# Gate and up as a 2x2 block product with seven products, and weight tiles of three k-tiles, in a streamed fp32 decoder layer

## The chip, the cores and the metric

The kernel runs on one core of a Trainium2 chip. The metric is the time of one execution in microseconds of the device; the time before is the median of three runs.

## The reference

One decoder layer on x of 256 tokens by 2048, all in fp32, with alpha = 2^(1/4):

```
x <- LN1(alpha*x + 0.5*SwiGLU_1(x))                  # D_FF = 5632
x <- LN2(alpha*x + W_out [DiffAttn(x @ W_in) || RWKV7(x @ W_in)])   # W_in: 2048 x 6432
x <- LN3(alpha*x + 0.5*SwiGLU_2(x))
swiglu(x, wg, wu, wd) = (silu(x @ wg) * (x @ wu)) @ wd
```

Almost all of the arithmetic is in the matrix products with w_gate, w_up (2048 x 5632 each), w_down (5632 x 2048), twice, and W_in and W_out.

## The kernel before

Tokens stand in two tiles of 128, called token tile 0 and 1 (`tt` in the code). An activation tile is transposed on PE and split into a high half in the reduced format fp32r and the remainder (`xh`, `xl`), and so is each weight tile (`wh`, `wl`). A product of a k-tile (128 rows of K) with a column block of 512 is three matmuls into one PSUM bank: xh*wh, xh*wl, xl*wh (L113, L114, L115).

Weights pass through once. A step of `Stream.block` loads two k-tiles of one column block (`raw`, 128x1024, on SP's DMA queue, L134), ACT rounds them to `wh` (L137), DVE subtracts to get `wl` (L138), and PE uses them first for token tile 0 and then, LAG steps later (4 in the FFNs, 2 in the mixer), for token tile 1. There are three `raw` buffers, and seven slots of `wh` and `wl` in the FFNs, five in the mixer. `raw` and five of these slots live in a pool `wp` that all stages share.

The stages are FFN1, the mixer ("mix") and FFN2. An FFN has eleven column blocks of gate and up, in halves of six and five. For each, a gate block is followed by an up block; `gate_done` takes Silu of the gate's bank on ACT (`sg`, L222), `up_done` multiplies on DVE (`h`, L227), PE transposes h (L230) and ACT and DVE split it (`hh`, L240, L241). After each half the down product runs over its k-tiles for four column blocks, and `down_done` adds into `y` (L264, L266). When a token tile's last block is there, `ln_tail` normalises it in four quarters on DVE (L193, L194); in the first two stages each quarter is transposed and split for the next stage (L75, L81, L82) and written to a DRAM tile `xs` on ACT's queue (L199), and in the last it goes to the output. The mixer begins with a block of 288 columns of W_in, and its attention and recurrence run beside the weight stream as background generators; its final product is with W_out.

Nothing in the code fixes the order of work on an engine: a scheduler that simulates the program when it is built sets each engine's order, and the pools' buffers decide which instruction has to wait for which.

## Time and profile before

| | |
|---|---|
| median of three runs | 2006.51 us (2006.06 to 2007.28) |
| profiled execution: its own span | 2006.8 us |
| PE busy | 1972.1 us (98%), 9671 matmuls |
| DVE busy | 1145.7 us (57%) |
| ACT busy | 885.0 us (44%) |
| DMA | 373.35 MB, mean 186 GB/s |

Busy times count an engine's own instructions and not those that only issue DMAs. A matmul's record is longer than the distance to the next one, since matmuls overlap; what one costs is the distance between starts. The page names the instruction that released a waiting one, and the chain is followed back from the end in this way.

### The profile page before, as it was taken

How to read it: one execution, taken by the hardware profiler on the slowest of the kernel's cores; microseconds unless marked ns; L12 is line 12 of the kernel's file. 1: busy time of each engine (PE TensorE's matmuls, PEld its weight loads, DVE VectorE, ACT ScalarE, POOL GpSimd, SP SyncE). 2: the span in 40 equal slices, each digit the busy share in tenths (PEclk: the TensorE clock that was granted, in tenths of full speed). 3: DMA queues.
4: the chain of work that ended last, by engine and by line, in shares of the span. 5: the costliest groups of instructions: out<-in, count | busy, mean ns of one | idle time of the engine just before them, and what ended most of it. 6: DMA issues, size and time to landing. Idle time of an engine off the chain costs nothing.

```text
span 2006.8 us, 24924 instructions
## 1 busy us (share of the span) xinstructions
PE 1972.1 (98%) x9671; PEld 1618.6 (81%) x9671; DVE 1145.7 (57%) x1419; ACT 885.0 (44%) x1096; POOL 34.2 (2%) x68
## 2 busy tenths in 40 slices
...
GB/s 243 220 188 189 187 191 206 211 192 230 190 188 189 195 167 192 155 160 171 137 123 147 187 117 171 210 200 189 189 188 190 206 211 191 230 190 188 190 195 128
DMA packets 202008, 373.35 MB, mean 186 GB/s; under 512 B 22826, under 2 KB 24944, under 8 KB 201120
## 3 DMA queue, kind: packets, MB, share of 16 engines
...
## 4 chain that ended last, share of the span: by engine, by line
PE 91%; DVE 4%; DMA 2%; ACT 1%; issue 1%; ACTq 0%; POOL 0%; DVEq 0%
PE acc L113 28%; PE acc L115 28%; PE acc L114 28%; DVE wl L138 1%; DMA raw<-in_ffn_w_gate_dram 1%; PE tr L230 1%; ACT wh L137 1%; DVE y L193 1%; DVE y L194 1%; PE sm L556 0%; PE tr L353 0%; DMA raw<-in_ffn_w_up_dram 0%; PE pr L498 0%; PE at L775 0%; PE tr L75 0%
## 5 line engine op out<-in xcount | busy, mean ns | idle before, releaser
L138 DVE TENSOR_TENSOR wl<-raw,wh 128x1024 fp32r<-128x1024 f32 (+1 forms) x665 | 807.9, 1217 | 649.1 <-ACT wh L137 648.4
L137 ACT CAST wh<-raw 128x1024 fp32r<-128x1024 f32 (+1 forms) x665 | 694.9, 1047 | 832.7 <-PE acc L115 728.3
L115 PE MATMUL acc<-wh,xl 128*128 128x512 f32 (+1 forms) x1952 | 740.6, 391 | 0.5 <-DVE xl L82 0.5
L114 PE MATMUL acc<-wl,xh 128*128 128x512 f32 (+1 forms) x1952 | 735.4, 392 | 3.9 <-DVE wl L138 3.9
L113 PE MATMUL acc<-wh,xh 128*128 128x512 f32 (+1 forms) x1952 | 728.1, 392 | 0.3 <-ACT xh L81 0.2
L114 PEld LDWEIGHTS acc<-wl,xh 128*128 128x128 f32 x1952 | 368.0, 189 | 80.0 <-DVE wl L138 5.2
L113 PEld LDWEIGHTS acc<-wh,xh 128*128 128x128 f32 x1952 | 368.2, 189 | 79.1 <-issue 3.0
L115 PEld LDWEIGHTS acc<-wh,xl 128*128 128x128 f32 x1952 | 367.8, 188 | 77.0 <-issue 2.3
L115 PE MATMUL acc<-wh,hh 128*128 128x512 f32 x704 | 254.5, 390 | 0.0
L114 PE MATMUL acc<-wl,hh 128*128 128x512 f32 x704 | 253.6, 389 | 0.0
L113 PE MATMUL acc<-wh,hh 128*128 128x512 f32 x704 | 252.6, 389 | 0.0
L114 PEld LDWEIGHTS acc<-wl,hh 128*128 128x128 f32 x704 | 132.1, 188 | 27.6
L115 PEld LDWEIGHTS acc<-wh,hh 128*128 128x128 f32 x704 | 132.2, 188 | 27.4
L113 PEld LDWEIGHTS acc<-wh,hh 128*128 128x128 f32 x704 | 132.1, 188 | 27.4
L241 DVE TENSOR_TENSOR hh<-tr,hh 128x512 fp32r<-128x512 f32 x44 | 30.4, 691 | 64.2 <-ACT hh L240 64.2
L240 ACT CAST hh<-tr 128x512 fp32r<-128x512 f32 x44 | 25.8, 586 | 91.2 <-PE tr L230 91.2
L227 DVE SCALAR_TENSOR_TENSOR h<-sg,acc 128x512 f32<-128x512 f32 x44 | 30.2, 687 | 34.9 <-PE acc L115 34.9
L222 ACT ACTIVATE sg<-acc 128x512 f32<-128x512 f32 x44 | 26.3, 598 | 42.9 <-PE acc L115 42.9
L230 PEld LDWEIGHTS tr<-ident,h 128*128 128x128 f32 x176 | 21.7, 140 | 6.3 <-DVE h L227 0.7
L230 PE MATMUL tr<-ident,h 128*128 128x128 f32 x176 | 26.4, 272 | 0.3 <-DVE h L227 0.3
L584 DVE TENSOR_TENSOR itmp<-U,Y 64x31 f32<-64x31 f32 (+15 forms) x62 | 20.5, 331 | 7.3 <-DMA U<-dU 5.9
L586 DVE TENSOR_TENSOR Y<-Y,itmp 64x31 f32<-64x31 f32 (+15 forms) x62 | 20.6, 332 | 1.4
...
## 6 DMA issues: line engine op xcount, KB each, us to landing
raw<-in_ffn_w_up_dram SPq DMA_DIRECT2D x176, 512.0 KB, 3.8
raw<-in_ffn_w_down_dram SPq DMA_DIRECT2D x176, 512.0 KB, 4.2
raw<-in_ffn_w_gate_dram SPq DMA_DIRECT2D x175, 512.0 KB, 3.9
raw<-in_w_in_dram SPq DMA_DIRECT2D x96, 512.0 KB, 3.7
raw<-in_w_out_dram SPq DMA_DIRECT2D x32, 512.0 KB, 4.2
xs<-y ACTq DMA_DIRECT2D x16, 256.0 KB, 3.1
rc<-xs ACTq DMA_DIRECT2D x16, 256.0 KB, 4.3
...
```

Source lines behind the costliest of these rows:

```text
L113: T.matmul(a, hi, wh[:, j, :w], start=(ki + j == 0), stop=False)
L114: T.matmul(a, hi, wl[:, j, :w], start=False, stop=False)
L115: T.matmul(a, lo, wh[:, j, :w], start=False, stop=(ki + j == last))
L137: SC.copy(out=wh[:, c, :w], in_=raw[:, c, :w])
L138: V.tensor_tensor(out=wl[:, c, :w], in0=raw[:, c, :w], in1=wh[:, c, :w].bitcast(F32), op=ALU.subtract)
L222: SC.activation(out=s, in_=acc, func=AF.Silu)
L227: V.scalar_tensor_tensor(out=h, in0=sg[tt], scalar=0.5, in1=acc, op0=ALU.mult, op1=ALU.mult)
L230: T.transpose(tr[:, i, :], h[:, i * P:(i + 1) * P], ident)
L240: SC.copy(out=hi, in_=tr)
L241: V.tensor_tensor(out=lo, in0=tr, in1=hi.bitcast(F32), op=ALU.subtract)
L584: V.tensor_tensor(out=tv, in0=U[:, 0:j, j:j + 1].to_broadcast([64, j, 32 - j]), in1=Y[:, j:j + 1, j:32].to_broadcast([64, j, 32 - j]), op= ...
L586: V.tensor_tensor(out=Y[:, 0:j, j:32], in0=Y[:, 0:j, j:32], in1=tv, op=ALU.add)
```

## The change

For every column block of an FFN but the first, `two_blocks` computes gate and up together. On k-tiles 0 to 5 it takes the 2x2 block product of (token tile 0, 1) x (k-tiles 0 to 2, 3 to 5) with (k-tiles 0 to 2, 3 to 5) x (gate, up) in the form with seven products instead of eight. Its operands are differences of weight tiles, made in place on the loaded tiles by DVE (L172, L176, L177, L188), and four sums and differences of the x tiles (`xsh`, `xsl`), made once in an FFN by `combinations` (L284 to L292). Sums of products are made in PSUM: bank `u` begins as a copy of `a` (L174) and `w` as a copy of `u` (L181), both by ACT; `z` is copied to SBUF as `s5` (L180) and DVE adds it to `u` in place (L184) and to `w` to give `v` (L186). The other ten k-tiles run as before into the four banks, `a` and `w` for the gate, `u` and `v` for up.

Around it, weight tiles are three k-tiles wide (128x1536) in the FFNs, apart from each FFN's first gate block; token tile 1 follows one step behind; there are four slots of `wh` and `wl` and eight of `raw`; `raw`, `wh` and `wl` live in each stage's own pool, so in the mixer and FFN2 they lie over tiles of the stage before; there are six accumulator banks and two for transposes; gamma and beta of the FFNs' norms are loaded into the tiles of x of token tile 1.

```diff
-LAG = {"ffn": 4, "mix": 2}
-NW = {"ffn": 7, "mix": 5}
-NRAW = 3
+LAG = {"ffn": 1, "mix": 2}
+NW = {"ffn": 4, "mix": 5}
+NRAW = {"ffn": 8, "mix": 3}
+WIDE = {"ffn": 3, "mix": 2}
+NACC = {"ffn": 6, "mix": 3}
...
-    wp = ctx.enter_context(tc.tile_pool(name="wp", bufs=1))
...
+        def load(self, src, r0, n, c0, w=NB, g=None):
+            raw = self.pool.tile([P, self.wide, NB], F32, tag="raw", name=nm("raw"), bufs=NRAW[self.name])
...
+        def halves(self, raw, n, w=NB, g=None):
...
+                SC.copy(out=wh[:, c, :w], in_=raw[:, c, :w])
+                V.tensor_tensor(out=wl[:, c, :w], in0=raw[:, c, :w], in1=wh[:, c, :w].bitcast(F32), op=ALU.subtract)
...
+        def two_blocks(self, srcs, c0, x, comb, done):
+            self.flush()
+            s0, s1 = srcs
+            a, z, u, w, v = (self.bank() for i in range(5))
+            A11, A12, A21, A22 = ((lambda j, t=t, k=k: x(t, k + j)) for t in range(2) for k in (0, 3))
+            r11 = self.load(s0, 0, 3, c0)
+            self.product(a, A11, 3, *self.halves(r11, 3), True, False)
+            r12 = self.load(s1, 0, 3, c0)
+            V.tensor_tensor(out=r11, in0=r12, in1=r11, op=ALU.subtract)
+            self.product(z, comb(0), 3, *self.halves(r11, 3), True, True)
+            SC.copy(out=u, in_=a)
+            r22 = self.load(s1, 3, 3, c0)
+            V.tensor_tensor(out=r12, in0=r22, in1=r12, op=ALU.subtract)
+            V.tensor_tensor(out=r11, in0=r22, in1=r11, op=ALU.subtract)
+            self.product(u, comb(1), 3, *self.halves(r11, 3), False, False)
+            s5 = self.pool.tile([P, NB], F32, tag="s5", name=nm("s5"))
+            SC.copy(out=s5, in_=z)
+            SC.copy(out=w, in_=u)
+            r21 = self.load(s0, 3, 3, c0)
+            self.product(a, A12, 3, *self.halves(r21, 3), False, False)
+            V.tensor_tensor(out=u, in0=u, in1=s5, op=ALU.add)
+            self.product(w, comb(2), 3, *self.halves(r12, 3), False, False)
+            V.tensor_tensor(out=v, in0=w, in1=s5, op=ALU.add)
+            self.product(u, comb(3), 3, *self.halves(r22, 3), False, False)
+            V.tensor_tensor(out=r11, in0=r21, in1=r11, op=ALU.subtract)
+            rest = [(6, 3), (9, 3), (12, 2), (14, 2)]
+            for i, (src, banks) in enumerate(((s0, (a, w)), (s1, (u, v)))):
+                for k, n in rest:
+                    raw = self.load(src, k, n, c0)
+                    h = self.halves(raw, n)
+                    for t in range(2):
+                        if i == 0 and k == 6 and t == 1:
+                            self.product(w, A22, 3, *self.halves(r11, 3), False, False)
+                        self.product(banks[t], lambda j: x(t, k + j), n, *h, False, k == 14)
+                        if k == 14:
+                            done(i, t, banks[t])
...
-                stream.block(wg, c0, NB, KX, x_lhs, gate_done)
-                stream.block(wu, c0, NB, KX, x_lhs, lambda tt, acc, j=j: up_done(tt, acc, j))
+                if j0 + j == 0:
+                    stream.block(wg, c0, NB, KX, x_lhs, gate_done, 2)
+                    comb = combinations()
+                    stream.block(wu, c0, NB, KX, x_lhs, lambda tt, acc, j=j: up_done(tt, acc, j))
+                    stream.flush()
+                else:
+                    stream.two_blocks((wg, wu), c0, x_lhs, comb, lambda i, tt, acc, j=j: up_done(tt, acc, j) if i else gate_done(tt, acc))
...
-                gb = load_gb(fp, lg, lb, "lng", "lnb", hT[(0, 0)][0][:, 0, 0:1].bitcast(F32))
+                gb = load_gb_over_x(lg, lb)
```

How the order of the engines changes is shown at three places. In the rows, the number behind a tile's name tells its buffers apart, and a wait names the engine or DMA queue whose semaphore is waited for.

PE in a gate block of FFN1 before; acc_224 is token tile 0's bank of one block, acc_238 the bank of the next:

```order
L113 MATMUL acc_238_1255<-wh_243_1287,xh_22_164 128x512 [waits Activation_49]
L113 MATMUL acc_224_1186<-wh_229_1212,xh_49_286 128x512
L114 MATMUL acc_224_1186<-wl_230_1213,xh_49_286 128x512
L115 MATMUL acc_224_1186<-wh_229_1212,xl_50_287 128x512
L113 MATMUL acc_224_1186<-wh_229_1212,xh_49_286 128x512
L114 MATMUL acc_224_1186<-wl_230_1213,xh_49_286 128x512
L114 MATMUL acc_238_1255<-wl_244_1288,xh_22_164 128x512 [waits DVE_49]
L115 MATMUL acc_238_1255<-wh_243_1287,xl_23_165 128x512
```

PE in the seven products after; acc_254 is the bank u, acc_255 the bank w, and the wait for ACT at w's first matmul is for the copy of u into w (L181), which itself waits for the row above it:

```order
L130 MATMUL acc_254_1410<-wh_264_1449,xsh_58_327 128x512
L131 MATMUL acc_254_1410<-wl_265_1450,xsh_58_327 128x512
L132 MATMUL acc_254_1410<-wh_264_1449,xsl_59_328 128x512
L130 MATMUL acc_255_1411<-wh_270_1481,xsh_58_327 128x512 [waits Activation_49]
L131 MATMUL acc_255_1411<-wl_271_1482,xsh_58_327 128x512 [waits DVE_49]
L132 MATMUL acc_255_1411<-wh_270_1481,xsl_59_328 128x512
```

Before, matmuls of two banks alternate where an operand is late; after, the nine matmuls of w stand directly behind the last of u.

DVE in the gate and up stage before:

```order
L138 TENSOR_TENSOR wl_327_1725<-raw_325_1723,wh_326_1724 128x1024 [waits DMAHW3_49,Activation_49]
L138 TENSOR_TENSOR wl_331_1744<-raw_329_1742,wh_330_1743 128x1024 [waits DMAHW4_49,Activation_49]
L227 SCALAR_TENSOR_TENSOR h_322_1707<-sg_294_1557,acc_298_1571 128x512 [waits PE_49]
L138 TENSOR_TENSOR wl_334_1762<-raw_332_1760,wh_333_1761 128x1024 [waits DMAHW5_49,Activation_49]
L138 TENSOR_TENSOR wl_337_1780<-raw_335_1778,wh_336_1779 128x1024 [waits DMAHW6_49,Activation_49]
L241 TENSOR_TENSOR hh_324_1714<-tr_323_1709,hh_324_1714 128x512 [waits Activation_49]
L138 TENSOR_TENSOR wl_343_1808<-raw_341_1806,wh_342_1807 128x1024 [waits DMAHW7_49,Activation_49]
```

DVE in the seven products after, from the second low half of a pair to the addition of s5 to u; raw_257, raw_260, raw_263 and raw_267 are the tiles r11, r12, r22 and r21, and the two h belong to the pair before:

```order
L123 TENSOR_TENSOR wl_262_1432<-raw_257_1413,wh_261_1431 128x1536 [waits Activation_49]
L305 SCALAR_TENSOR_TENSOR h_246_1382<-sg_232_1294,acc_198_1104 128x512 [waits PE_49]
L177 TENSOR_TENSOR raw_257_1413<-raw_263_1445,raw_257_1413 128x1536 [waits DVE_49]
L305 SCALAR_TENSOR_TENSOR h_249_1398<-sg_233_1302,acc_200_1106 128x512 [waits PE_49]
L123 TENSOR_TENSOR wl_269_1468<-raw_267_1465,wh_268_1467 128x1536 [waits DMAHW6_49,Activation_49]
L123 TENSOR_TENSOR wl_265_1450<-raw_257_1413,wh_264_1449 128x1536 [waits Activation_49]
L123 TENSOR_TENSOR wl_271_1482<-raw_260_1428,wh_270_1481 128x1536 [waits PE_49,Activation_49]
L188 TENSOR_TENSOR raw_257_1413<-raw_267_1465,raw_257_1413 128x1536 [waits DVE_49]
L123 TENSOR_TENSOR wl_273_1496<-raw_263_1445,wh_272_1495 128x1536 [waits PE_49,Activation_49]
L319 TENSOR_TENSOR hh_248_1389<-tr_247_1384,hh_248_1389 128x512 [waits Activation_49]
L319 TENSOR_TENSOR hh_251_1405<-tr_250_1400,hh_251_1405 128x512 [waits Activation_49]
L184 TENSOR_TENSOR acc_254_1410<-acc_254_1410,s5_266_1462 128x512 [waits Activation_49]
```

Before, low halves alternate with the h and hh of the pair before; after, differences of weight tiles and an addition in PSUM stand among them, and the next nine matmuls of u (PE) wait for the last row.

SP's queue at the border from FFN1 to the mixer before:

```order
L134 DMA raw_973_5300<-in_ffn1_w_down_dram 128x2x512 [waits DMAHW5_49,DVE_49]
L134 DMA raw_1006_5467<-in_w_in_dram 128x2x288 [waits DMAHW6_49,DVE_49]
L134 DMA raw_1010_5480<-in_w_in_dram 128x2x288 [waits DMAHW7_49,DVE_49]
L134 DMA raw_1013_5492<-in_w_in_dram 128x2x288 [waits DMAHW0_49,DVE_49]
L134 DMA raw_1017_5511<-in_w_in_dram 128x2x288 [waits DMAHW1_49,DVE_49]
L134 DMA raw_1020_5529<-in_w_in_dram 128x2x288 [waits DMAHW3_49,DMAHW2_49,DVE_49]
```

SP's queue at the same place after; raw_886 lies over token tile 0's y and raw_890 over token tile 1's, and the DMA queues that these two rows wait for are those of the writes of xs0 and of xs1:

```order
L114 DMA raw_853_5053<-in_ffn1_w_down_dram 128x3x512 [waits DMAHW2_49,DVE_49]
L114 DMA raw_886_5208<-in_w_in_dram 128x2x288 [waits DMAHW1_49,DMAHW2_49,DMAHW0_49,DMAHW7_49,DVE_49,PE_49]
L114 DMA raw_890_5221<-in_w_in_dram 128x2x288 [waits DMAHW4_49,DMAHW5_49,DMAHW3_49,DMAHW6_49,DVE_49,PE_49]
L114 DMA raw_893_5233<-in_w_in_dram 128x2x288
L114 DMA raw_897_5252<-in_w_in_dram 128x2x288 [waits DMAHW7_49,DVE_49]
L114 DMA raw_900_5270<-in_w_in_dram 128x2x288 [waits DMAHW0_49,DVE_49]
```

Before, the first loads of W_in wait only for buffers of the weight stream; after, they stand behind the end of each token tile's norm and the writes of its result. On PE the matmuls of W_in's first block come after all 32 transposes of the two token tiles, where before they were mixed with them.

At the border to FFN2, PE before, from the first transposes of token tile 0's y:

```order
L75 MATMUL at_1909_10044<-ident_76,y_1707_9153 128x128 [waits DVE_49]
L75 MATMUL at_1909_10044<-ident_76,y_1707_9153 128x128 x3
L75 MATMUL sm_1912_10056<-ident_76,y_1707_9153 128x128 [waits DVE_49,PE_49]
L75 MATMUL sm_1912_10056<-ident_76,y_1707_9153 128x128 x3
L113 MATMUL acc_1944_10185<-wh_1942_10180,xh_1910_10049 128x512 [waits Activation_49]
L75 MATMUL at_1915_10068<-ident_76,y_1708_9154 128x128 [waits DVE_49]
L75 MATMUL at_1915_10068<-ident_76,y_1708_9154 128x128 x3
L75 MATMUL sm_1918_10080<-ident_76,y_1708_9154 128x128 [waits DVE_49,PE_49]
L75 MATMUL sm_1918_10080<-ident_76,y_1708_9154 128x128 x3
L114 MATMUL acc_1944_10185<-wl_1943_10181,xh_1910_10049 128x512 [waits DVE_49]
L115 MATMUL acc_1944_10185<-wh_1942_10180,xl_1911_10050 128x512 [waits DVE_49]
L113 MATMUL acc_1944_10185<-wh_1942_10180,xh_1910_10049 128x512
```

and after, from the last transposes of token tile 1's y:

```order
L76 MATMUL sm_1808_9874<-ident_73,y_1587_8894 128x128 [waits DVE_49,PE_49]
L76 MATMUL sm_1808_9874<-ident_73,y_1587_8894 128x128 x3
L76 MATMUL at_1811_9886<-ident_73,y_1588_8895 128x128 [waits DVE_49,PE_49]
L76 MATMUL at_1811_9886<-ident_73,y_1588_8895 128x128 x3
L76 MATMUL sm_1814_9898<-ident_73,y_1588_8895 128x128 [waits DVE_49,PE_49]
L76 MATMUL sm_1814_9898<-ident_73,y_1588_8895 128x128 x3
L130 MATMUL acc_1822_9924<-wh_1820_9920,xh_1790_9790 128x512 [waits Activation_49]
L130 MATMUL acc_1826_9943<-wh_1820_9920,xh_1806_9867 128x512
L131 MATMUL acc_1822_9924<-wl_1821_9921,xh_1790_9790 128x512 [waits DVE_49]
L132 MATMUL acc_1822_9924<-wh_1820_9920,xl_1791_9791 128x512
L130 MATMUL acc_1822_9924<-wh_1820_9920,xh_1790_9790 128x512
L131 MATMUL acc_1822_9924<-wl_1821_9921,xh_1790_9790 128x512
```

Before, matmuls of FFN2's first gate block follow the first transposes of token tile 0; after, the first of them follows the last transposes of token tile 1, and the second waits for a low half (wl_1821) that stands on DVE behind seven of the combinations of x.

127 lines of the change are left out of this document (79 added, 48 removed).

## The prediction

> **What bounds the kernel now.** I read the page's busy shares and its chain first, then a table of stretches, then the timeline of each engine at the stage borders. The page's busy line, with the share of the span in brackets, and the chain by engine and line:
>
> ```profile
> PE 1972.1 (98%) x9671; PEld 1618.6 (81%) x9671; DVE 1145.7 (57%) x1419; ACT 885.0 (44%) x1096; POOL 34.2 (2%) x68
> PE 91%; DVE 4%; DMA 2%; ACT 1%; issue 1%; ACTq 0%; POOL 0%; DVEq 0%
> ```
>
> PE is the path, so a matmul taken away shortens the span unless something new stands in its place. The stretches below are a gate/up stretch of FFN1, the border from FFN1 to the mixer, the mixer, the border to FFN2, and the tail (stretch and its length, then busy us of PE, PEld, DVE, ACT, POOL, granted clock, DMA share, GB/s):
>
> ```profile
> 100.00:270.00 170.00, 170.00 (x765) 140.66 (x764) 85.11 (x77) 73.55 (x78) 0.00 (x0) 1.00 0.66 189
> 730.00:760.00 30.00, 25.30 (x137) 22.18 (x136) 24.08 (x43) 9.79 (x16) 2.04 (x2) 0.89 0.46 146
> 760.00:1240.00 480.00, 470.65 (x2949) 377.12 (x2949) 340.40 (x634) 258.68 (x441) 11.23 (x12) 0.98 0.53 156
> 1240.00:1270.00 30.00, 26.17 (x104) 20.41 (x103) 28.34 (x42) 9.39 (x11) 2.00 (x2) 0.83 0.58 175
> 1990.00:2006.80 16.80, 4.85 (x22) 3.69 (x20) 12.32 (x20) 0.00 (x0) 2.01 (x2) 0.80 0.38 125
> ```
>
> In gate/up PE never waits, with DVE half idle and DMA at two thirds; time is lost only at borders and ends. So the change takes work off the bound, and what counts is what it puts in PE's way.
>
> **1. Matmuls removed.** A gate/up pair before is 16 k-tiles x 2 token tiles x 2 matrices x 3 = 192 matmuls. After, six k-tiles take 7 products of 9 (63 for 72), so 183. Twenty pairs (two FFNs, eleven each, the first of each left as it was): 180 fewer. Two neighbouring pairs' h on DVE, and eight transposes in a row on PE, give the price:
>
> ```profile
> 139.05 0.69 DVE L227 SCALAR_TENSOR_TENSOR h<-sg,acc 128x512 f32<-128x512 f32 x1 [1.31 <-PE acc L115]
> 183.54 0.69 DVE L227 SCALAR_TENSOR_TENSOR h<-sg,acc 128x512 f32<-128x512 f32 x1 [1.31 <-PE acc L115]
> 740.90 1.03 PE L75 MATMUL tr<-ident,y 128*128 128x128 f32 x8
> ```
>
> (183.54 - 139.05 - 1.03) / 192 = 0.2264 us a matmul; 180 x 0.2264 = **-40.8 us**, 2.04 a pair. All of it lies on the path.
>
> **2. What stands in its place in each pair.** Rows for the new work (line, engine, shapes, count, busy us, mean ns, idle before); the second row serves for back-to-back work, the third is an add out of PSUM, the fourth a 384-wide operation:
>
> ```profile
> L138 DVE TENSOR_TENSOR wl<-raw,wh 128x1024 fp32r<-128x1024 f32 x655 | 800.7, 1224 | 648.7 <-ACT wh L137 648.0
> L194 DVE SCALAR_TENSOR_TENSOR y<-y,rs,lnb 128x512 f32<-128x512 f32 x24 | 16.7, 747 | 0.0
> L266 DVE TENSOR_TENSOR y<-y,acc 128x512 f32<-128x512 f32 x16 | 10.9, 684 | 17.0 <-PE acc L115 17.0
> L777 DVE SCALAR_TENSOR_TENSOR s<-dist,at 128x384 f32<-128x384 f32 x16 | 8.4, 544 | 2.4 <-PE at L775 2.4
> L137 ACT CAST wh<-raw 128x1024 fp32r<-128x1024 f32 x655 | 688.2, 1052 | 816.4 <-PE acc L115 718.1 <-DMA raw<-in_ffn_w_gate_dram 31.8 <-DMA raw<-in_ffn_w_up_dram 26.1
> L349 ACT COPY tm<-acc 128x512 f32<-128x512 f32 x20 | 11.7, 587 | 10.3 <-PE acc L115 10.1
> ```
>
> 512 columns more cost DVE 1.224 - 0.684 = 0.54, so a 128x1536 instruction is put at 1.77 on DVE, and on ACT at 1.05 + (1.05 - 0.59) = 1.5.
>
> *The copy w<-u (L181).* PE's queue has the nine matmuls of w right behind the last of u. The copy can't begin before that last matmul is out, nor w before the copy. The end of the kernel shows the first latency (PE's last matmul of token tile 0, DVE's use of it), and that border of FFN2 the second (wl's end at 1262.11, PE's start):
>
> ```profile
> 1987.66 0.39 PE L115 MATMUL acc<-wh,hh 128*128 128x512 f32 x1
> 1988.09 0.69 DVE L266 TENSOR_TENSOR y<-y,acc 128x512 f32<-128x512 f32 x1 [5.62 <-PE acc L115]
> 1994.46 0.39 PE L115 MATMUL acc<-wh,hh 128*128 128x512 f32 x1
> 1995.24 0.68 DVE L266 TENSOR_TENSOR y<-y,acc 128x512 f32<-128x512 f32 x1
> 1999.69 2.73 DVE L194 SCALAR_TENSOR_TENSOR y<-y,rs,lnb 128x512 f32<-128x512 f32 x4
> 1260.90 1.21 DVE L138 TENSOR_TENSOR wl<-raw,wh 128x1024 fp32r<-128x1024 f32 x1
> 1262.17 0.80 PE L114 MATMUL acc<-wl,xh 128*128 128x512 f32 x1 [0.55 <-DVE wl L138]
> ```
>
> 0.43 from start to reader, 0.59 copy, 0.06 to PE, less the 0.23 that a matmul takes anyway: 0.85 us idle a pair. Unseen is a copy with both ends in PSUM: as low as 0.3 (half), as high as 1.05 if read and write take turns, so 0.56 to 1.3; I take the row. Queued behind the copy on ACT are casts that PE needs 3 us later; u<-a (L174) and s5<-z (L180) hide under z's nine matmuls and the transposes (3 us), and without that cover u<-a would cost another 0.85.
>
> *DVE's chain.* Per pair DVE now has 15 instructions of 1536 (11 low halves, 4 differences), 4 of 1024, 2 adds, 4 for h: 26.6 + 4.9 + 1.4 + 2.8 = 35.6 us against 16 x 1.22 + 2.8 = 22.4 before. That fits in some 43, but the seven products hold 21.5 of it against 63 x 0.2264 = 14.3 of PE. With four slots DVE can start some 42 matmuls (9.5 us) ahead of the pair. Back to back an instruction costs less (at 1999.69, four in 2.73 where one takes 0.747: 0.08 less each after the first). From the slot: a cast 1.5, ten 1536-wide at 1.72 (between 1.77 and 1.69), five 512-wide at 0.64 up to u += s5 (L184): -9.5 + 21.9 = 12.4. PE asks for it after 46 matmuls, 1.03 of transposes and 0.85 of wait: 12.3. I add 0.2 for a match so close: stall 1.05 a pair, **+21 us**; ends 0.56 (+11) and, with the add at 1.22 and DVE's wide instructions 4% longer, 2.25 (+45).
>
> *At nothing:* three-wide loads (eight raw buffers give the 9.5 us lead; a row's 3.9 us for 512 KB is 5.9 for 768 KB), hidden by the rest's 120 matmuls; the down phases, whose DVE and ACT load is as before; FFN1's combinations, beside the first up block (0 +/- 2).
>
> **3. Border FFN1 to mixer.** Rows of PE, DVE and SP's queue before, and three of the DMA list (KB, us to landing):
>
> ```profile
> 724.39 23.87 SPq L134 DMA_DIRECT2D raw<-in_w_in_dram  x8
> 740.67 0.39 PE L115 MATMUL acc<-wh,hh 128*128 128x512 f32 x1
> 748.55 0.29 PE L115 MATMUL acc<-wh,xl 128*128 128x288 f32 x1
> 752.28 1.09 PE L75 MATMUL tr<-ident,y 128*128 128x128 f32 x4 [3.43 <-DVE y L194]
> 754.04 0.68 DVE L82 TENSOR_TENSOR xl<-tr,xh 128x512 fp32r<-128x512 f32 x1
> 764.69 0.29 PE L114 MATMUL acc<-wl,xh 128*128 128x288 f32 x1
> 765.22 0.29 PE L115 MATMUL acc<-wh,xl 128*128 128x288 f32 x1
> raw<-in_ffn_w_gate_dram SPq DMA_DIRECT2D x175, 512.0 KB, 3.9
> raw<-in_w_in_dram SPq DMA_DIRECT2D x96, 512.0 KB, 3.7
> xs<-y ACTq DMA_DIRECT2D x16, 256.0 KB, 3.1
> ```
>
> X = 741.06 is FFN1's last matmul. Before, w_in was issued at X-16.7, 31 of its 96 matmuls ran ahead of token tile 1's transposes, and the block ended at X+24.3. After, w_in's first load waits for the writes of xs0 and the second for those of xs1 (raw lies over y), and every matmul of it follows all 32 transposes. Token tile 0's sum now has 14 matmuls behind it, not 30, so it comes at X - 0.39 - 14 x 0.2264 + 0.43 = X-3.1. Two norms of 7.15 (1988.09 to 1995.24) and four splits of 0.6 between end at X+13.6; the last write lands 3.2 later, X+16.8, the second load 3.4 after that (288 columns, so under the row's 3.7), X+20.2; with a cast and low half, 1.5, and the 84 matmuls that then remain at 0.13 (764.69 to 765.22 is four) the block ends at X+33: **+8.5 us** (5 if the writes land sooner, 11 with the cold clock below).
>
> **4. Border mixer to FFN2.** PE and SP's queue before:
>
> ```profile
> 1241.13 23.70 SPq L134 DMA_DIRECT2D raw<-in_ffn_w_gate_dram  x8
> 1253.29 0.39 PE L115 MATMUL acc<-wh,xl 128*128 128x512 f32 x1
> 1256.72 1.12 PE L75 MATMUL at<-ident,y 128*128 128x128 f32 x4 [3.04 <-DVE y L194]
> 1264.64 0.63 PE L113 MATMUL acc<-wh,xh 128*128 128x512 f32 x1
> 1266.26 0.40 PE L114 MATMUL acc<-wl,xh 128*128 128x512 f32 x1
> 1269.16 2.73 DVE L194 SCALAR_TENSOR_TENSOR y<-y,rs,lnb 128x512 f32<-128x512 f32 x4
> 1273.03 0.48 PE L115 MATMUL acc<-wh,xl 128*128 128x512 f32 x1
> ```
>
> Y = 1253.68. Before, 33 matmuls are done when full speed is back at 1273.03: as if FFN2 began at 1273.03 - 33 x 0.2264 = Y+11.9. The second norm ended at 1271.89, Y+18.2, with four low halves (4.9 us) and the gaps they make among its operations; after, the waits of the gate loads take them out, so I put its end at Y+12.2. Transposes and split take 2.2, seven combination operations on DVE (L284 to L288; two of 512, two of 256, three of 384) some 3.5 by the rows of 0.684 and 0.544, one low half 1.2: Y+19.1; cold matmuls (ten from 1262.17 to 1266.26 took 1.8 more than 10 x 0.2264) make it Y+20.6: **+8.7 us** (5 to 11).
>
> **5. End.** Token tile 0's sum came 30 matmuls ahead of PE's end (1987.66 to 1994.46); with 14, the DVE chain of two norms starts 16 x 0.2264 later against it: **+3.6 us**.
>
> **Sum:** -40.8 + 21 + 8.5 + 8.7 + 3.6 = +1.0 against the profiled 2006.8, which stands 0.3 above the median of 2006.51: 2007.5.
>
> **Rivals.** *Faster: w's wait is short.* With the copy at 0.3, w waits 0.56, and PE asks for the add at 12.0; DVE's chain is there at 12.1 if each wide instruction takes the low 1.69. At 0.6 a pair, 12 in all, -40.8 + 12 + 8.5 + 8.7 + 3.6 = -8: 1998.5 (1992 with the borders at 5 each). For it: the copy doesn't leave PSUM, which no row shows. Against it: 512 columns cost ACT 0.587, and all the rows of DVE that read PSUM are as long as those that don't. The Trainium skill, "ScalarE: Activation LUTs", notes that ScalarE writes PSUM faster than SBUF; it gives no figure, and by it the sum would lie between this and 2007.5.
>
> *Slower: DVE sets the pace of the seven products.* It decides once the chain ends past 12.3, on the add at L184 and then at the low halves behind it. At 2.25 a pair: 24 more, 2032. For it: the margin is 0.1 us of 22; against it: half of DVE's time is free in this stage.
>
> *Slower: the clock.* The 3.04 and 3.43 us gaps are followed by matmuls of 0.63 and a clock of 0.83 to 0.89; 1.8 us lost each. If each pair's new gap did that, 20 x 1.8 = 36 more: 2044. Against it: the mixer has 9.35 us of small gaps and keeps 0.98. The Trainium skill, "TensorE: Matmul & The Clock Gate", section "A second HAM failure mode: psum-queue depth-cycling", says that PE's short idles between groups of matmuls can make the clock swing; its section "HAM oscillation — how this bites in real kernels" asks for gaps over about 3.4 us. The trace's 3.04 us gap was enough, its small gaps were not; by the first section the time would be this rival's, by the second the sum's.
>
> **How the numbers follow.** The sum 0.52 (its own range 1999 to 2017, from a stall of 0.85 to 1.3 and the borders' ends); the short wait 0.20; DVE 0.20; clock 0.06; else 0.02. Predicted 2007.5. The range 1994 to 2032 leaves out the clock, half of the DVE case and the lowest of the short wait. No change is 0.2%, 4 us, about what a measurement can tell. Half of the sum's chance lies within it, a fifth below, the rest above: faster 0.10 + 0.20 = 0.30, same 0.26, slower 0.16 + 0.20 + 0.06 + 0.02 = 0.44.
>
> **What would show it.** A pair's period of 44.49 - 2.04 + 1.05 = 43.5 us between neighbouring h; PE idle near 0.85 us once a pair in front of w's first matmul, released by ACT L181, and less than 0.4 in front of u's last nine, released by DVE L184; the 288-wide block ending near X+33; clock 1.00 in gate/up. A period under 43.1 or over 44.4, or w_in loads landing ahead of the norm's end, makes the prediction wrong.

## The result, and the profile after

| | before | after |
|---|---|---|
| median of three runs | 2006.51 us (2006.06 to 2007.28) | 2017.31 us (2016.46 to 2018.40) |
| profiled execution, its span | 2006.8 us | 2015.2 us |
| mean granted clock of that execution | 0.990 | 0.983 |

The ratio is 1.0056, with an interval of 1.0038 to 1.0074: slower by about half a per cent, where the sum said no change (the chances named slower as the likeliest way, with 0.44). The medians differ by 10.8 us, the two profiled executions by 8.4; the rest of this text accounts for the 8.4, which the sum had put at 1.0.

The page's busy line of the kernel after (busy us, share of the span, instructions):

```profile
PE 1944.6 (96%) x9491; PEld 1585.4 (79%) x9491; DVE 1377.2 (68%) x1477; ACT 971.0 (48%) x1078; POOL 43.5 (2%) x76
```

The 180 matmuls are gone (9671 to 9491), and PE's busy time fell by 27.5 us while the span grew by 8.4, so PE now idles 36 us more. Where, the same kind of table of stretches shows (gate and up of FFN1, the border to the mixer, and ten microseconds of FFN2's first two-block pair):

```profile
100.00:270.00 170.00, 167.36 (x749) 136.87 (x748) 129.01 (x97) 94.78 (x89) 0.00 (x0) 1.00 0.60 204
730.00:760.00 30.00, 20.65 (x102) 17.12 (x101) 22.45 (x37) 9.90 (x16) 1.86 (x2) 0.66 0.53 166
1330.00:1340.00 10.00, 9.34 (x27) 6.84 (x27) 6.36 (x6) 5.17 (x5) 0.00 (x0) 0.62 0.59 186
```

In gate and up PE idles 2.6 us of 170 at full clock. The border's granted clock is 0.66 where it was 0.89. The third stretch is one that the prediction had no term for: 27 matmuls in 10 us, at a granted clock of 0.62.

**A pair in the steady state.** From the timeline of the kernel after, token tile 0's h of two neighbouring pairs on DVE; then, within one pair, PE's last matmul of `u`, ACT's copy, PE's first matmul of `w`, DVE's add to `u` (L184), PE's first use of `u` behind it and the next matmul (in brackets: idle before, and who ended it):

```profile
98.32 0.68 DVE L305 SCALAR_TENSOR_TENSOR h<-sg,acc 128x512 f32<-128x512 f32 x1
141.79 0.68 DVE L305 SCALAR_TENSOR_TENSOR h<-sg,acc 128x512 f32<-128x512 f32 x1
...
151.50 0.39 PE L132 MATMUL acc<-wh,xsl 128*128 128x512 f32 x1
151.92 0.57 ACT L181 COPY acc<-acc 128x512 f32<-128x512 f32 x1 [1.42 <-PE acc L132]
152.54 0.50 PE L130 MATMUL acc<-wh,xsh 128*128 128x512 f32 x1 [0.66 <-ACT acc L181]
154.20 0.69 DVE L184 TENSOR_TENSOR acc<-acc,s 128x512 f32<-128x512 f32 x1
154.95 0.49 PE L130 MATMUL acc<-wh,xsh 128*128 128x512 f32 x1
155.28 0.39 PE L131 MATMUL acc<-wl,xsh 128*128 128x512 f32 x1
```

The period is 141.79 - 98.32 = 43.47 us, against 44.49 before. From the start of `u`'s last matmul to `w`'s first are 1.04 us; without the copy it would be one pitch, 0.23, so the copy costs 0.81 a pair. The next matmul starts 0.11 late (0.34 behind `w`'s first), and so does the one behind `u`'s first (155.28, 0.33 behind 154.95); with these it is 1.02 in all. DVE's add ends at 154.89, 0.06 ahead of PE's start on `u`, and no idle time is shown there. The waits over the whole run, and the groups of the copy and of the three-wide low half:

```profile
PE acc L130 <- ACT acc L181: 13.2, 20, 0.7
PE acc L131 <- DVE wl L123: 10.0, 6, 2.8
```

```profile
L123 DVE TENSOR_TENSOR wl<-raw,wh 128x1536 fp32r<-128x1536 f32 x340 | 591.7, 1754 | 360.4 <-ACT wh L122 359.4
L181 ACT COPY acc<-acc 128x512 f32<-128x512 f32 x20 | 11.4, 570 | 28.5 <-PE acc L132 28.5
```

There are twenty waits of 0.66 for the copy, one in each pair, and the copy itself takes 0.57, about as long as ACT's copies from PSUM to SBUF. The 10.0 us for low halves, in six waits, are something else: none is in a steady pair. Two are in FFN2's first block and its first two-block pair (2.84 and 2.77), two in the mixer (2.17 and 1.14), one in FFN1's first two-block pair (0.85) and one at the first border (0.21).

**Border FFN1 to mixer.** PE's last matmul of FFN1, SP's issue of the first W_in loads, the first matmul of the 288-wide block, and its last:

```profile
730.62 0.39 PE L132 MATMUL acc<-wh,hh 128*128 128x512 f32 x1
738.91 29.27 SPq L114 DMA_DIRECT2D raw<-in_w_in_dram  x14
748.17 0.85 PE L130 MATMUL acc<-wh,xh 128*128 128x288 f32 x2 [1.25 <-ACT wh L122]
764.41 0.29 PE L132 MATMUL acc<-wh,xl 128*128 128x288 f32 x1
```

With X = 730.62 + 0.39 = 731.01, the loads go out at X+7.9 instead of X-16.7, no matmul of W_in runs before X+17, and the block ends at X+33.7.

**Border mixer to FFN2.** PE's last matmul of the mixer, the first gate matmuls, the first low half on DVE, and the matmul that waited for it:

```profile
1250.53 0.39 PE L132 MATMUL acc<-wh,xl 128*128 128x512 f32 x1
...
1266.57 1.22 PE L130 MATMUL acc<-wh,xh 128*128 128x512 f32 x2 [1.62 <-ACT wh L122]
1269.36 1.22 DVE L123 TENSOR_TENSOR wl<-raw,wh 128x1024 fp32r<-128x1024 f32 x1
1270.63 0.80 PE L131 MATMUL acc<-wl,xh 128*128 128x512 f32 x1 [2.84 <-DVE wl L123]
```

Two matmuls run, and then PE stands 2.84 us more for a low half that DVE makes behind the combinations.

**FFN2's first two-block pair.** DVE: the difference that makes `u`'s operand (L177), what DVE does behind it, the last DVE row being `u`'s own low half; then PE's first two matmuls of `u`:

```profile
1320.35 1.75 DVE L177 TENSOR_TENSOR raw<-raw,raw 128x1536 f32<-128x1536 f32 x1
1322.01 1.75 DVE L123 TENSOR_TENSOR wl<-raw,wh 128x1536 fp32r<-128x1536 f32 x1
...
1324.28 1.75 DVE L123 TENSOR_TENSOR wl<-raw,wh 128x1536 fp32r<-128x1536 f32 x1
...
1326.55 1.75 DVE L123 TENSOR_TENSOR wl<-raw,wh 128x1536 fp32r<-128x1536 f32 x1
...
1325.07 0.50 PE L130 MATMUL acc<-wh,xsh 128*128 128x512 f32 x1 [1.39 <-ACT wh L122]
1328.35 0.80 PE L131 MATMUL acc<-wl,xsh 128*128 128x512 f32 x1 [2.77 <-DVE wl L123]
```

Two low halves for later products stand on DVE ahead of the one that PE needs. PE waits 1.39 and 2.77 us with one matmul between them, and of the matmuls behind them sixteen start 0.43 us after the one before instead of 0.23. The pair takes 51.86 us, from token tile 1's h to the next (1318.08 to 1369.94).

**End.** PE's last matmul and DVE's last norm operations:

```profile
1999.98 0.39 PE L132 MATMUL acc<-wh,hh 128*128 128x512 f32 x1
...
2008.68 2.73 DVE L249 SCALAR_TENSOR_TENSOR y<-y,rs,lngb 128x512 f32<-128x512 f32 x4
```

PE's end is 2000.37, the span's 2015.2: 14.8 us of tail instead of 11.95.

The first or last PE row of each stage, read as above in each profile, gives a table in us. Y is the mixer's last matmul; "period" is the steady distance of neighbouring pairs in FFN1. The kernels under the second row are those of the next section.

| kernel | start to X | X to end of 288 block | mixer from there to Y | Y to PE's end | PE's end to span's end | span | period |
|---|---|---|---|---|---|---|---|
| before | 741.06 | 24.45 | 488.17 | 741.17 | 11.95 | 2006.8 | 44.49 |
| after | 731.01 | 33.69 | 486.22 | 749.45 | 14.83 | 2015.2 | 43.47 |
| plain_pairs | 740.30 | 34.00 | 496.02 | 749.86 | 14.82 | 2035.0 | 44.48 |
| copy_twice | 773.57 | 33.77 | 491.03 | 789.25 | 14.78 | 2102.4 | 47.95 |
| w_fresh | 737.41 | 33.65 | 497.51 | 752.27 | 14.86 | 2035.7 | 43.93 |
| pool_differences | 783.89 | 33.88 | 490.26 | 798.45 | 14.82 | 2121.3 | 48.6 |
| own_pools | 741.47 | 31.38 | 496.31 | 748.07 | 11.97 | 2029.2 | 44.49 |
| lag_one | 740.37 | 24.38 | 489.29 | 740.70 | 15.86 | 2010.6 | 44.49 |
| order_fix | 732.40 | 33.32 | 494.96 | 744.25 | 14.87 | 2019.8 | 43.5 |
| late_combinations | 731.57 | 33.73 | 486.53 | 746.23 | 14.84 | 2012.9 | 43.47 |
| two_wide | 725.67 | 24.21 | 493.81 | 732.62 | 11.49 | 1987.8 | 43.05 |
| two_wide_four_slots | 749.36 | 30.23 | 489.75 | 756.44 | 16.22 | 2042.0 | 45.1 to 45.5 |
| two_wide_late | 726.42 | 24.40 | 493.94 | 732.97 | 11.47 | 1989.2 | 43.05 |

So after against before: -10.0 in FFN1, +9.2 at its border, -1.9 in the mixer, +8.3 in FFN2, +2.9 at the end.

**A caution for every total below.** The mixer's code is the same in nearly all of these kernels, and its time runs from 486 to 498 us. Each edit, wherever it is, lets the scheduler choose other orders there too. Totals are therefore compared with the mixer's column beside them, and the verdicts go by stages. The columns of stages that an edit doesn't touch agree within about 1 us (288 block 33.3 to 34.0, end 14.78 to 14.87), which is the resolution of the table.

### The profile page after: what moved, and what is told of

It is laid out like the page before. It is cut to its first block, busy times and chain, and to the rows that moved or that the text cites. A ratio compares the mean times of both kernels' runs of the same rounds, so it can differ in the third digit from the quotient of the medians.

```text
span 2015.2 us, 24059 instructions
## 1 busy us (share of the span) xinstructions
PE 1944.6 (96%) x9491; PEld 1585.4 (79%) x9491; DVE 1377.2 (68%) x1477; ACT 971.0 (48%) x1078; POOL 43.5 (2%) x76
## 5 line engine op out<-in xcount | busy, mean ns | idle before, releaser
L123 DVE TENSOR_TENSOR wl<-raw,wh 128x1536 fp32r<-128x1536 f32 (+3 forms) x585 | 881.8, 1522 | 511.9 <-ACT wh L122 510.0
L122 ACT CAST wh<-raw 128x1536 fp32r<-128x1536 f32 (+3 forms) x585 | 750.7, 1294 | 802.4 <-PE acc L132 638.0
L131 PE MATMUL acc<-wl,xh 128*128 128x512 f32 (+1 forms) x1652 | 644.2, 392 | 6.4 <-DVE wl L123 6.4
L132 PE MATMUL acc<-wh,xl 128*128 128x512 f32 (+1 forms) x1652 | 641.4, 390 | 0.0
L130 PE MATMUL acc<-wh,xh 128*128 128x512 f32 (+1 forms) x1652 | 636.0, 393 | 3.1 <-ACT wh L122 3.1
L131 PEld LDWEIGHTS acc<-wl,xh 128*128 128x128 f32 x1652 | 312.0, 189 | 72.6 <-DVE wl L123 8.3
L130 PEld LDWEIGHTS acc<-wh,xh 128*128 128x128 f32 x1652 | 312.4, 189 | 69.9 <-ACT wh L122 4.9
L131 PEld LDWEIGHTS acc<-wl,hh 128*128 128x128 f32 x704 | 132.1, 188 | 27.5
L130 PE MATMUL acc<-wh,xsh 128*128 128x512 f32 x240 | 100.6, 419 | 14.6 <-ACT acc L181 13.2
L131 PE MATMUL acc<-wl,xsh 128*128 128x512 f32 x240 | 95.4, 398 | 3.6 <-DVE wl L123 3.6
L132 PE MATMUL acc<-wh,xsl 128*128 128x512 f32 x240 | 95.2, 397 | 0.0
L300 ACT ACTIVATE sg<-acc 128x512 f32<-128x512 f32 x44 | 26.2, 599 | 20.3 <-PE acc L132 20.2
L172 DVE TENSOR_TENSOR raw<-raw,raw 128x1536 f32<-128x1536 f32 x20 | 35.2, 1758 | 0.7
```

What stands on the lines that cost most here:

```text
L122: SC.copy(out=wh[:, c, :w], in_=raw[:, c, :w])
L123: V.tensor_tensor(out=wl[:, c, :w], in0=raw[:, c, :w], in1=wh[:, c, :w].bitcast(F32), op=ALU.subtract)
L130: T.matmul(a, hi, wh[:, j, :w], start=first and j == 0, stop=False, skip_group_check=True)
L131: T.matmul(a, hi, wl[:, j, :w], start=False, stop=False, skip_group_check=True)
L132: T.matmul(a, lo, wh[:, j, :w], start=False, stop=last and j == n - 1, skip_group_check=True)
L172: V.tensor_tensor(out=r11, in0=r12, in1=r11, op=ALU.subtract)
```

## The experiments

Ratios are to the runs of the kernel before on the same chip (medians 2008.3 to 2008.7 us), with a 95% interval.

### What the seven products are worth: plain_pairs

The kernel after with its pools, widths, slots and lag, but all pairs computed with nine products of nine.

```diff
-stream.two_blocks((wg, wu), c0, x_lhs, comb, lambda i, tt, acc, j=j: ...)
+stream.block(wg, c0, NB, KX, x_lhs, gate_done)
+stream.block(wu, c0, NB, KX, x_lhs, lambda tt, acc, j=j: up_done(tt, acc, j))
```

> The changed kernel with each pair computed as an ordinary gate block and an ordinary up block (192 matmuls), everything else as changed: weight tiles three wide, buffers in each stage's own pool, lag 1. Theory (the seven products gain 1.02 us in a steady pair, 44.49 to 43.47, and lose 1.3 and 7.4 us in the first pair of FFN1 and of FFN2; the rest of the loss is in the borders and the end): a period of 44.5 us, and 2015.2 + 18 x 1.02 - 8.7 = 2025, some 2 us less because the combinations of x no longer stand in front of FFN2's first low half: 2021 to 2027. Rival (the wide tiles or the four slots cost time inside each pair as well): a period over 44.8 and more than 2031. Rival (the seven products lose more than they gain as they stand): 2015 or less.

Measured 2034.55 us, 1.0125 (1.0103 to 1.0147). The period is back at 44.48, FFN1 is 9.3 us longer than after, FFN2 only 0.4. The total lies above what was expected because of the mixer, 9.8 us longer than after; it falls where the first rival put it, but that rival needed a period over 44.8. By stages: what the change puts around the products costs 9.5 us at the first border, 8.7 in FFN2 and 2.9 at the end, with not one product saved; the products then earn 9.3 in FFN1 and next to nothing in FFN2.

### The wait for the copy: copy_twice, w_fresh, pool_differences

copy_twice makes the copy w<-u twice:

```diff
             SC.copy(out=w, in_=u)
+            SC.copy(out=w, in_=u)
```

> The changed kernel with the copy of u into w (L181) issued twice in a row on ACT. Theory (this copy lies on PE's path in each pair): the wait in front of w's first matmul grows from 0.66 to about 1.15 us, the additions at L184 are then no longer late (0.1 us), so 0.4 to 0.5 us a pair: 2023 to 2025.5. Rival (DVE's chain up to L184 is the later of the two and sets the pace): the pair's period stays within 0.1 us of 43.47, 2015 to 2017.

Measured 2101.31 us, 1.0459 (1.0437 to 1.0481): 4.5 us a pair, far from what a second copy takes. ACT's rows behind the first copy, which began at 160.17, and PE's rows in the same pair say why:

```profile
160.65 2.85 ACT L122 CAST wh<-raw 128x1536 fp32r<-128x1536 f32 x2
163.40 0.59 ACT L182 COPY acc<-acc 128x512 f32<-128x512 f32 x1
...
162.18 0.49 PE L130 MATMUL acc<-wh,xh 128*128 128x512 f32 x1 [2.05 <-ACT wh L122]
164.04 0.50 PE L130 MATMUL acc<-wh,xsh 128*128 128x512 f32 x1 [1.36 <-ACT acc L182]
```

The scheduler put two casts between the two copies. PE waited 2.05 and 1.36 us, and seven of the next ten matmuls came every 0.43 us, which together is 4.5. It is no clean doubling: it shows that ACT's place in the path is `w`'s start, and that what stands ahead of the copy on ACT counts as much as the copy.

w_fresh takes the seed away: `w` is started by its own product, `u` is copied to SBUF, and DVE adds it to `w` later.

```diff
-            SC.copy(out=w, in_=u)
+            uc = self.pool.tile([P, NB], F32, tag="sg", name=nm("uc"), bufs=2)
+            SC.copy(out=uc, in_=u)
...
-            self.product(w, comb(2), 3, *self.halves(r12, 3), False, False)
+            self.product(w, comb(2), 3, *self.halves(r12, 3), True, True)
+            V.tensor_tensor(out=w, in0=w, in1=uc, op=ALU.add)
```

> The changed kernel with w begun by its own product instead of a copy of u: ACT copies u to SBUF, DVE adds that copy to w after the product (one addition more a pair on DVE), so w's first matmul waits for nobody. Theory (DVE's chain up to the addition at L184 ends 0.1 us behind the copy, so the wait moves there): no idle time in front of w, about 0.9 us in front of u's last nine matmuls released by DVE, period 43.3 to 43.9, time 2011 to 2024. Rival (only the copy costs, DVE has slack): period 42.6, 2015.2 - 17 = 1998.

Measured 2036.56 us, 1.014 (1.0117 to 1.0162); period 43.93, so half a microsecond a pair *longer* than after, though the wait of 0.66 is gone. PE's rows and DVE's add to `u` in one pair:

```profile
157.28 0.50 PE L130 MATMUL acc<-wh,xh 128*128 128x512 f32 x1 [0.25 <-ACT wh L122]
157.31 0.69 DVE L185 TENSOR_TENSOR acc<-acc,s 128x512 f32<-128x512 f32 x1
158.05 0.50 PE L130 MATMUL acc<-wh,xsh 128*128 128x512 f32 x1 [0.27 <-DVE acc L185]
```

PE now waits for a cast and for the add (L185 is L184 of after) instead of the copy, and gains nothing: in both kernels the add starts 12.41 us after the pair's first h, and PE starts on `u` at 13.15. This is the prediction's "match so close" of DVE's chain with PE: take one wait away and the other appears in its place, as long. So the 0.81 of the copy is no price that could be saved by itself. The half microsecond more comes behind it. Four matmuls there (160.31 to 162.92) start 0.05 to 0.11 late, and DVE's low halves stand behind the one more add; that this add is the reason is likely and not tried by itself. The total lies above the 2011 to 2024 expected because the mixer, too, is 11.3 us longer than after.

pool_differences is w_fresh with two of the four weight differences on POOL, to shorten DVE's chain:

```diff
-            V.tensor_tensor(out=r12, in0=r22, in1=r12, op=ALU.subtract)
+            G.tensor_tensor(out=r12, in0=r22, in1=r12, op=ALU.subtract)
...
-            V.tensor_tensor(out=r11, in0=r21, in1=r11, op=ALU.subtract)
+            G.tensor_tensor(out=r11, in0=r21, in1=r11, op=ALU.subtract)
```

> The w_fresh kernel (w's first matmul waits for no copy) with two of the four differences of weight tiles (L176 and L188 of the changed kernel) on POOL instead of DVE, so that DVE's chain up to the addition to u is two instructions of 1.75 us shorter. Theory (in the changed kernel the copy and DVE's chain end within 0.1 us of each other, and only taking away both frees PE): steady period 42.5 to 42.8 instead of 43.47 (43.93 with the copy alone taken away). Rival (POOL needs so long for a difference that the casts behind it come late, or slows DVE): period 43.4 or more. The times of POOL are in no trace so far; below 5 us a difference the theory holds.

Measured 2123.48 us, 1.0572 (1.0550 to 1.0593), period about 48.6. Groups of the two subtractions and of DVE's low half, and the wait of PE for the add, in this kernel:

```profile
L190 POOL TENSOR_TENSOR raw<-raw,raw 128x1536 f32<-128x1536 f32 x20 | 96.7, 4835 | 151.7 <-issue 119.3 <-DVE wl L123 32.4
L176 POOL TENSOR_TENSOR raw<-raw,raw 128x1536 f32<-128x1536 f32 x20 | 70.1, 3507 | 660.9 <-DVE raw L172 639.4 <-DVE neglam L430 21.5
L123 DVE TENSOR_TENSOR wl<-raw,wh 128x1536 fp32r<-128x1536 f32 x340 | 692.6, 2055 | 411.4 <-ACT wh L122 410.6
```

```profile
PE acc L130 <- DVE acc L185: 75.6, 20, 4.2
```

A subtraction takes 3.5 to 4.8 us on POOL where DVE takes 1.76, and DVE's own low halves grow from 1754 to 2055 ns in the mean. So the chain got longer, and PE waits 3.8 us a pair for the add. DVE's chain is what binds once the copy is out of the way; that it is *just* as long as PE's path with the copy is a coincidence of this form. What a shorter chain would give stays open, since this edit lengthened it.

### The borders and the end: own_pools, lag_one

own_pools is the kernel before with `raw` and all slots in each stage's own pool instead of the shared one, nothing else:

```diff
-                raw = wp.tile([P, n, NB], F32, tag="raw", name=nm("raw"), bufs=NRAW)
-                pool = wp if self.slot < NW["mix"] else self.pool
+                raw = self.pool.tile([P, n, NB], F32, tag="raw", name=nm("raw"), bufs=NRAW)
+                pool = self.pool
```

> The kernel before with one part of the change: raw, wh and wl in each stage's own pool instead of a pool that all stages share (sizes, counts, lag 4 and the plain gate and up blocks as before). Theory (the pools make the border losses: nothing of the next stage's weights can be loaded, rounded or multiplied until the stage before has given up its tiles): the 288-wide block ends 30 to 34 us after FFN1's last matmul instead of 24.4; from the mixer's last matmul to PE's end 747 to 751 us instead of 741.2; pairs at 44.49; together 12 to 18 us, 2019 to 2025 against a profiled 2006.8, with up to 10 us more or less from the mixer, whose order the scheduler shuffles with every edit (486 to 497 us for the same code so far). Rival (the border losses come from the lag, the wide tiles or the combinations): 24 to 26 us and 741 to 743.

Measured 2030.79 us, 1.0112 (1.0093 to 1.0130). SP's issue of the first W_in loads and the first matmuls with them, X = 741.47:

```profile
744.78 12.54 SPq L133 DMA_DIRECT2D raw<-in_w_in_dram  x4
...
756.19 0.85 PE L112 MATMUL acc<-wh,xh 128*128 128x288 f32 x2 [3.60 <-ACT wh L136]
```

No matmul of W_in is left ahead of the transposes, and the block ends at X+31.4, 6.9 us later than before; FFN2 is 6.9 us longer too; period and end are unchanged. So three quarters of the first border's loss in the kernel after (6.9 of 9.2), and most of the second's (6.9 of 10.7, by the sum further down), come from the pools alone. (Another 8.1 us of this kernel's loss are in the mixer; one wait there, 5.3 us for `xh`, is seen in it and not in the kernel after. Whether the pools or a chance of the order put it there stays open.)

lag_one is the kernel before with token tile 1 one step behind, not four:

```diff
-LAG = {"ffn": 4, "mix": 2}
+LAG = {"ffn": 1, "mix": 2}
```

> The kernel before with the FFNs' lag between the token tiles 1 instead of 4 and nothing else. Theory (the lag sets how much of the norm of token tile 0 hides behind PE): from PE's last matmul to the end of the span 14.5 to 15.5 us instead of 11.95; the 288-wide block ends 25 to 28 us after FFN1's last matmul; pairs at 44.49; 2009 to 2014. Rival (the norm of token tile 1 alone sets the end): 12 us, 2006 to 2008.

Measured 2013.05 us, 1.0026 (1.0017 to 1.0036). The tail is 15.86 us, 3.9 more, as long as the prediction's 16 matmuls x 0.2264 = 3.6 and a little. The 288 block stays at 24.38, though it was expected to be late too: with the loads already there, the norm's later start costs the border nothing, and the lag counts at the end alone.

### FFN2's first pair and its first block: order_fix, late_combinations

order_fix lets the low halves of r12 and r22 be issued only after `u`'s. The casts stand in the same block of code, but in this run ACT kept their order and distances:

```diff
             self.product(u, comb(1), 3, *self.halves(r11, 3), False, False)
+            after_u = self.low.ins
...
+            with tc.issue_after(after_u):
+                h12 = self.halves(r12, 3)
+            self.product(w, comb(2), 3, *h12, False, False)
```

and the same for r22.

> The changed kernel with one rule more for the scheduler: on DVE the low halves for w's and u's last products come after the low half for u's first one. In the steady pairs they stand so already; in FFN2's first pair they stood the other way round, and PE waited 1.39 and 2.77 us there and then ran at a clock of 0.62. Theory (that order is what cost 8.4 us in FFN2's first pair): it takes 44 to 46 us instead of 51.9, 2007 to 2010. Rival (DVE is behind after the border whatever its order, or the clock falls anyway): 50 us and more, 2013 to 2016.

Measured 2025.11 us, 1.0078 (1.0058 to 1.0098), with 8.7 us more in the mixer than after. FFN2 is 5.2 us shorter, and its first two-block pair takes 47.7 us instead of 51.86, between the 44 to 46 of the theory and the rival's 50. The two waits in that pair are now:

```profile
1333.81 0.50 PE L130 MATMUL acc<-wh,xsh 128*128 128x512 f32 x1 [1.38 <-ACT wh L122]
1335.60 0.80 PE L131 MATMUL acc<-wl,xsh 128*128 128x512 f32 x1 [1.29 <-DVE wl L123]
```

The wait for the low half went from 2.77 to 1.29, the one for the cast stayed, and five matmuls came every 0.43 us instead of sixteen. So DVE's order, and the clock behind its gap, are shown as the cause of 4.2 of the pair's 8.4 us above the steady period: 1.5 is the shorter wait, and by the difference the clock is 2.7. For the rest (L177 itself, which stood behind another low half, and ACT's cast) the order is the likely cause, not tried further.

late_combinations issues the combinations only after the first gate block's last low half:

```diff
-                    comb = combinations()
+                    with tc.issue_after(stream.low.ins):
+                        comb = combinations()
```

> The changed kernel with the combinations of x kept behind the first gate block's last low half on DVE. Theory (seven of them stand in front of FFN2's first low half, 3.5 us, of which 2 to 4 are on the path): FFN2's first h comes 63.5 to 65.5 us after the mixer's last matmul instead of 67.6, and the first seven-product pair is not slower than its 51.9 us. Rival (the path there is the loads or ACT's roundings, or the combinations are then late for the first pair): 66.5 and more, or a first pair longer by what was gained.

Measured 2016.03 us, 1.0036 (1.0024 to 1.0048). The first gate matmuls, shown above for the kernel after, now read

```profile
1267.48 1.22 PE L130 MATMUL acc<-wh,xh 128*128 128x512 f32 x2 [1.62 <-ACT wh L122]
```

with no wait of 2.84 behind them; PE's transposes of FFN2's first h come 64.49 us after Y instead of 67.56, and the stage is 3.2 shorter. The first two-block pair keeps its 51.67.

### A version that beats both: two_wide and two of its parts

two_wide keeps the seven products, on four of sixteen k-tiles with two-wide tiles, so that 186 matmuls of 192 stay in a pair instead of 183. In exchange it keeps LAG 4, seven slots, and the shared pool for five slots and three of six `raw`.

```diff
-LAG = {"ffn": 1, "mix": 2}
-NW = {"ffn": 4, "mix": 5}
-NRAW = {"ffn": 8, "mix": 3}
-WIDE = {"ffn": 3, "mix": 2}
+LAG = {"ffn": 4, "mix": 2}
+NW = {"ffn": 7, "mix": 5}
+NRAW = {"ffn": 6, "mix": 3}
+WIDE = {"ffn": 2, "mix": 2}
...
-            raw = self.pool.tile([P, self.wide, NB], F32, tag="raw", name=nm("raw"), bufs=NRAW[self.name])
+            raw = (wp if i < NRAW["mix"] else self.pool).tile([P, self.wide, NB], F32, tag=f"raw{i}", name=nm("raw"))
...
+            pool = wp if self.slot < NW["mix"] else self.pool
...
-            rest = [(6, 3), (9, 3), (12, 2), (14, 2)]
+            rest = [(k, 2) for k in range(4, 16, 2)]
```

> Seven products as in the changed kernel but on k-tiles 0 to 3 in tiles two k-tiles wide (186 matmuls a pair instead of 183), with the buffers of the kernel before: a shared pool for raw and the first five slots, seven slots and lag 4 in the FFNs, and three raw tiles more there. Theory (the wait for the copy and DVE's chain cost time because four slots leave PE no other work; here the scheduler puts 18 matmuls of bank a between u's last and w's first matmul, and the borders are covered again): no idle time in front of w, period 44.49 - 6 x 0.2264 = 43.1 us, the 288-wide block 24 to 26 us after FFN1's last matmul, 1976 to 1992. Rival (the copy and the additions cost the same 1.02 us a pair whatever the slots): period 44.1, 1996 to 2010.

Measured 1989.96 us (1988.69 to 1991.45), 0.9906 (0.9892 to 0.9921): faster than before by 18 us, and the fastest kernel here. Its stretch in gate and up, two neighbouring pairs' h, and SP's issue at the first border (X = 725.67):

```profile
100.00:270.00 170.00, 170.00 (x768) 141.14 (x767) 119.33 (x111) 92.66 (x104) 0.00 (x0) 1.00 0.65 205
...
140.12 1.28 DVE L310 SCALAR_TENSOR_TENSOR h<-sg,acc 128x512 f32<-128x512 f32 x2
183.18 1.28 DVE L310 SCALAR_TENSOR_TENSOR h<-sg,acc 128x512 f32<-128x512 f32 x2
...
700.84 27.03 SPq L118 DMA_DIRECT2D raw<-in_w_in_dram  x8
```

PE does not idle in the stretch. The period is 43.06, 1.43 below before, where six matmuls are 6 x 0.2264 = 1.36: the whole saving arrives. The scheduler has other matmuls, 18 by the trace, to put between `u`'s last and `w`'s first, so the copy is hidden. W_in is loaded 24.8 us ahead of X, the 288 block ends at X+24.2 and the tail is 11.5 us, both as before. In FFN2 the gain is 8.6 us, less than the ten pairs' 14. There the first transposes wait for the norm on DVE, 5.27 us in this row of PE and 3.04 in the kernel before, and the first gate block ends 5.8 us later after Y, and this version leaves that as it is:

```profile
1248.96 1.12 PE L77 MATMUL at<-ident,y 128*128 128x128 f32 x4 [5.27 <-DVE y L254]
```

two_wide_four_slots takes away the slots and the lag again:

```diff
-LAG = {"ffn": 4, "mix": 2}
-NW = {"ffn": 7, "mix": 5}
+LAG = {"ffn": 1, "mix": 2}
+NW = {"ffn": 4, "mix": 5}
```

> The two_wide kernel with four slots and lag 1 in the FFNs as in the changed kernel, instead of seven and 4; all else as in two_wide. Theory (slots give DVE and ACT their lead and the scheduler other matmuls to put into the wait): with four slots of two k-tiles PE waits again in the seven products, for the low halves or the addition, 0.3 to 1 us a pair, period 43.4 to 44.1. Rival (the narrower tiles alone remove the wait, since DVE's chain is shorter by a third): period 43.05 as with seven slots.

Measured 2044.29 us, 1.0180 (1.0158 to 1.0202). The period is 45.1 to 45.5, worse than before the change. PE's waits in one pair:

```profile
153.98 0.50 PE L135 MATMUL acc<-wh,xsh 128*128 128x512 f32 x1 [0.34 <-DVE acc L189]
162.85 0.73 PE L135 MATMUL acc<-wh,xh 128*128 128x512 f32 x2 [0.60 <-ACT wh L127]
```

A slot holds only 12 matmuls of PE in the rest and 6 in the products, so four of them let DVE and ACT run less far ahead, and PE waits for both. The effect, over 2 us a pair, is twice and more what was expected: the look-ahead is what makes two_wide work. Of the two edits the slots act in the pairs; the lag enters only the plain blocks, since `two_blocks` gives each tile to both token tiles at once.

two_wide_late adds late_combinations' edit to two_wide.

> The two_wide kernel with the combinations of x kept behind the first gate block's last low half on DVE, as in late_combinations. Theory (it took 3 us from FFN2's border there): FFN2's first h comes 1 to 3 us earlier than 60.6 us after the mixer's last matmul, the rest of FFN2 as in two_wide; 1984 to 1990 with the mixer's scatter. Rival (with the weights loaded ahead the border is set by the norm alone): no change beyond the mixer's.

Measured 1991.15 us, 0.9917 (0.9898 to 0.9935): no change. With the shared pool the gate block's loads and casts stand ahead of the norm, and the combinations delay nothing.

## Why the prediction was right or wrong

The forecast was 2007.5 us and no change; the time was 2017.3, inside the range, on the slower side, by none of the three rivals. That it lies inside is partly luck: the room above 2007.5 was kept for a longer stall, slower borders and DVE's pace, and most of what filled it was a stretch that had no term.

- **The pairs: right.** Forecast -0.99 a pair (-2.04 and +1.05), measured -1.02. The wait for the copy was put at 0.85 and is 0.81, by the same latencies: 0.42 to the copy's start, 0.57 copy, 0.05 to PE. The 0.2 for DVE's close match is seen as two matmuls 0.11 late, behind `w`'s first and `u`'s first, and not as a wait; but w_fresh shows that the chain is as near as it was reckoned, and that PE comes no earlier to `u` without the copy. FFN1 as a whole came out at -10.0 for -9.9, partly by luck: nine pairs make 9 x 1.02 = 9.2, the first two-block pair took 45.75 and lost 1.3, and 2.1 us were gained elsewhere in the stage, which I haven't placed.
- **Border FFN1 to mixer: right.** +8.5 forecast, +9.2 measured, the block's end at X+33.7 for X+33. own_pools shows 6.9 of it to be the pools alone. In the rest of the walk two misses nearly cancel: the cast of the second load starts at 750.11, X+19.1, where its landing had been put at X+20.2, and the twelve matmuls from 750.84 to 753.88 take 3.04 us instead of 12 x 0.13 = 1.6, a slow clock that the sum had left to the range.
- **Border mixer to FFN2: 2 us short.** Take the first h of token tile 1 less its lag of 24 matmuls (5.44) before: 1315.55 - 5.44 - 1253.68 = 56.4 us after Y; after the change it is 1318.08 - 1250.92 = 67.2. That is +10.7 for +8.7. The walk on DVE holds: the first low half ends at 1269.36 + 1.22, Y+19.7, for Y+19.1, and late_combinations gives back 3.1 us of the 3.5 that the combinations were put at. Of the other 1.4, 1.2 is the slow clock behind it: the thirteen matmuls up to 1276.31 take 1276.31 - 1270.63 = 5.68 us, where 13 x 0.2264 is 2.94, so 2.7 too much, and the sum had 1.5 for it.
- **End: right.** +3.6 forecast, +2.9 measured; lag_one alone +3.9.
- **The step that failed: the stall of 1.05 was taken for all twenty pairs.** It was walked for a pair in the steady state, with the slots full ahead of it. FFN2's first two-block pair comes behind the border with another order on DVE, and takes 51.86 us: 8.4 above the steady period. This one pair is more than the 7.4 us between the sum and the profiled time (+1.0 and +8.4). order_fix takes 4.2 of it away with a change of DVE's order alone.
- **The clock rival** was right in kind and wrong in place. In the steady pairs the gaps of 0.66 us every 43 leave the granted clock at 1.00. The Trainium skill's "TensorE: Matmul & The Clock Gate", section "A second HAM failure mode: psum-queue depth-cycling", tells of a clock that swings because PE is idle for short times, and often, between groups of matmuls; for gaps as rare as these the trace shows no such swing. In FFN2's first pair 1.39 and 2.77 us with one matmul between are followed by a granted clock of 0.62. In order_fix 1.38 and 1.29 were enough for five slow matmuls, below the gap of about 3.4 us for which the section "HAM oscillation — how this bites in real kernels" of that page of the Trainium skill asks; the measurements decide here. The prediction also took the mixer's 0.98 as a sign that small gaps leave the clock alone. It is a mean: in the kernel before the clock falls twice in that stretch, behind a gap of 2.17 us (1033.48) and behind gaps of 0.48 and 1.49 us close together (1178.70 and 1180.63).
- **The faster rival** (a short copy inside PSUM) is refuted: 570 ns against 587 out to SBUF. **The rival of DVE's pace** did not come about in the kernel after, where DVE's chain and the copy tie; in w_fresh PE waits for DVE, but for 0.27 us and not for the rival's 2.25.
- **The mixer**, put at nothing, gave 1.9 us, within what its order scatters.

Forecast and measured by terms, in us: FFN1 -9.9 and -10.0; border +8.5 and +9.2; mixer 0 and -1.9; FFN2 with its border -1.2 and +8.3; end +3.6 and +2.9; together +1.0 and +8.4. Only FFN2 is off by more than 2.
